# Split order of the seven-product MLP: block 6 loaded and split ahead of block 5

## The chip, the cores and the metric

The kernel runs on one core of one Trainium2 chip. The metric is device time in microseconds (us), the median of the runs shown. Beside the runs there is one profiled execution, whose trace all rows and durations here come from. The engines are TensorE (PE; PEld are its weight loads), VectorE (DVE), ScalarE (ACT), GpSimd (POOL) and SyncE (SP), which issues most DMAs.

## The reference

One layer of an encoder trunk on 512 rows of 1024 features: a mixer, a cross attention, and an MLP. The change is in the MLP alone:

```python
    u = rmsnorm(h, norm_ff_g[l]) @ w1[l]              # (512 x 1024) @ (1024 x 4096)
    h = h + jnp.square(jax.nn.relu(u)) @ w2[l]        # (512 x 4096) @ (4096 x 1024)
return rmsnorm(h, final_norm_g)
```

## The kernel before

The MLP's 4096 hidden features are cut into eight groups of 512. Group 0's up projection is computed in the plain way, which is the last thing before the loop that the change touches. For groups 1 to 7 (`SEVEN`) the up projection (`mlp_up7`), and for all groups the down projection (`mlp_down`), is a 2 x 2 block product made of **seven products** in place of eight. They are named 1 to 7, and TensorE computes them in the order of `PRODUCTS`: 1, 5, 6, 2, 7, 3, 4. In the loop a group's up stage comes first, then the down stage of the group before it; the last two groups share one down stage.

Every factor is held as two float32r tiles, a high part and the rest (`hi`, `lo`), and a product of factors is three matmuls: hi by hi, hi by the activations' rest, lo by hi. So each product of an up stage is 4 row blocks x 2 column halves x 3 = 24 matmuls of 128x256, and the third of them is the first that reads the weights' `lo`. A down stage has seven products of 12 matmuls of 128x512.

A **unit** is one weight block made ready for one product. `load` (line 1329) issues its DMA from SyncE into a raw tile `wru` (up) or `wrd` (down): for products 1, 2 and 3 straight from the weights, for 5, 6 and 7 from `wsu`/`wsd`, sums of blocks that GpSimd's adding DMAs ("presums", line 445, paced by TensorE's progress) have put into memory earlier. `prep` (line 1346) splits it: ScalarE copies it to `whu` (line 181), VectorE computes `wlu` = raw - `whu` (line 185). Product 4 has no load of its own: once block 6 is split, GpSimd adds a further block into the same raw tile (line 1356, the **adding DMA**), and that tile, split again, is block 4. Raw tiles, `wh`/`wl` tiles and PSUM banks are few, so a load or split often waits for an older tile's last reader.

In the up stage three PSUM banks hold the products: `uU` takes 1, then is copied to `uV` (line 1421) and takes 6 on top; `uY` takes 5, is saved as `y5` (line 1424), then overwritten with the sum in `uU` (`uY<-uU`, line 1426, after product 6) for product 3; `uU` takes 7 on top, VectorE reads it (`sq<-uU,y`, line 1430), and product 4 goes on top of it after that. So product 6 cannot start before the copy to `uV`, product 7 not before the copy `uY<-uU`, and product 4 not before line 1430.

`hidden_part` splits the hidden activations for the down stage into `hb` tiles (lines 1491 to 1495): `hb27` is group 2's for product 7. `hidden_sums` (lines 1476 to 1479) makes their sums `s5`, `n6`, `s3`, `s7` after product 4 of the up stage. `add_to` (lines 1508, 1510) adds down products to `acc`.

The order of the instructions on TensorE is the program's. On the other engines a scheduler sets it when the kernel is built, from the program's order, its own estimate of when operands are ready, and priorities: `ahead(PW)` raises or lowers an instruction's priority, `keep_in_program_order` fixes its place among its engine's instructions as written. Once built, each engine runs its queue strictly in that order, SyncE's DMA issues included. In the kernel before, block 4's split of the up stage and the copy `uY<-uU` are both kept in the program's order.

Of the kernel before, what the change touches and what calls it, by code (L numbers as in the profile page):

```python
# [12 lines left out]
AF = mybir.ActivationFunctionType  # L13
# [33 lines left out]
def emit(  # L47
# [21 lines left out]
    nc = tc.nc  # L69
    te, ve, ac, gp = nc.tensor, nc.vector, nc.scalar, nc.gpsimd  # L70
# [26 lines left out]
    def s4(shape, name, dt=F32):  # L97
        return s4p.tile([P] + shape, dt, tag="s4", name=name)

    def k4(shape, name, dt=F32):  # L100
        return k4p.tile([P] + shape, dt, tag="k4", name=name)
# [7 lines left out]
    def t2(name, dt=F32, shape=(S,)):  # L109
        return t2p.tile([P] + list(shape), dt, tag="t2", name=name)  # L110
# [6 lines left out]
    def mm(name, shape=(S,)):  # L117
        return mmp.tile([P] + list(shape), F32, tag="mm", name=name)
# [4 lines left out]
    def sc(name, shape=(S,)):  # L123
        return scp.tile([P] + list(shape), F32, tag="sc", name=name)
# [46 lines left out]
    def new_parts(shape, name):  # L171
        pad = [P, UK * (UW + FH)]
        hi = whp.tile([P, shape[0] * shape[1]], R, tag="wh", name=f"wh{name}", padded_shape=pad)
        lo = wlp.tile([P, shape[0] * shape[1]], R, tag="wl", name=f"wl{name}", padded_shape=pad)
        return [t.rearrange("p (k n) -> p k n", k=shape[0]) for t in (hi, lo)]

    def split_of(hi, lo, raw):
        def split(what="hl"):
            at = None
            if "h" in what:  # L180
                at = ac.activation(hi, raw, AF.Copy)  # L181
            if "v" in what:
                ve.tensor_copy(hi, raw)
            if "l" in what:
                ve.tensor_tensor(lo, raw, f(hi), ALU.subtract)  # L185
            return at

        return split
# [26 lines left out]
    def load_next(parts=2, between=None):  # L215

        i = len(stream)
        if i >= len(specs):
            return []
        units, splits = [], []  # L220
        uk = specs[i][0][1].shape[1] // 2
        for n in range(2):
            note = None if between is None else (lambda q, n=n: between(n * parts // 2 + q))
            unit, some = load_unit(f"{i}{'ab'[n]}", specs[i], slice(n * uk, (n + 1) * uk), parts // 2, note)
            units.append(unit)
            splits += some
        stream.append(tuple([u[x] for u in units] for x in range(2)))
        return splits
# [60 lines left out]
    def ahead(n):  # L289

        return tc.high_priority(offset=n) if n else nullcontext()
# [64 lines left out]
    first = load_next(4, more_x)  # L356
# [298 lines left out]
    for hp in range(2):  # L655
        wt = next_panel()
        for j in range(2):
            h = 2 * hp + j
            ps = mm(f"gq{h}")
# [124 lines left out]
    for li, m in enumerate(mlev):  # L784
# [8 lines left out]
        for hp in range(2):  # L793
# [3 lines left out]
            ps = sc(f"lv{hp}{m}", (NT, 2, w))  # L797
# [507 lines left out]
    for i in range(2):  # L1305
        gp.dma_start(gfin[i], final_norm_g[i * S : (i + 1) * S].partition_broadcast(P))
    HS = S // 2
    units, raws, unit_q = {}, {}, deque()
    sqs, comb, hbs = {}, {}, {}
    PRODUCTS = ("1", "5", "6", "2", "7", "3", "4")  # L1310
    QUAD = {"1": "00", "2": "10", "3": "11"}
    raw_n = [0]

    def raw_tile(name):
        raw_n[0] += 1
        if raw_n[0] % RAWS == 3:
            return t4(f"wr{name}")
        if raw_n[0] % RAWS in (0, 2):
            return wrp.tile([P, D], F32, tag="wr", name=f"wr{name}", padded_shape=[P, UK * UW])
        return s4([D], f"wr{name}")  # L1320
# [3 lines left out]
    def add_unit(key, shape):  # L1324

        kind, g, part = key[:3]
        name = "".join(map(str, key))
        block = block1 if kind == "u" else block2
        box = []

        def load():
            if part == "4":
                box.append(raws.pop((kind, g)))
                return
            if part == "6":
                raw = raws[kind, g] = s4(shape, f"wr{name}")
            else:
                raw = raw_tile(name).rearrange("p (k n) -> p k n", k=shape[0])
            if part in SUMS:
                src = wsum[kind, g, part]  # L1340
            else:
                src = block(g, QUAD[part])
            nc.sync.dma_start(raw, src)
            box.append(raw)

        def prep():
            while not box:
                load_q.popleft()()
            unit = new_parts(shape, name)
            late = (kind, part) == ("u", "4")  # L1350
            with ahead(0 if late else PW):
                split = split_of(unit[0], unit[1], box[0])()
                if late:
                    tc.keep_in_program_order(split)
            if part == "6":
                tc.keep_in_program_order(gp.dma_start(box[0], block(g, "10"), accum_op=ALU.add))  # L1356
            units[key] = unit

        unit_q.append((key, prep))
        load_q.append(load)  # L1360

    def up_units(g):
        for part in PRODUCTS:
            add_unit(("u", g, part), [UK, WT])

    def down_units(gs):
        for name in PRODUCTS:
            for g in gs:
                add_unit(("d", g, name), [2, S])

    def unit(*key):

        while key not in units:
            unit_q.popleft()[1]()
        got = units[key]
        at = order.index(key)
        while unit_q and len(order) - len(unit_q) < at + 4:
            unit_q.popleft()[1]()
        while load_q and len(order) - len(load_q) < at + LOADS:
            load_q.popleft()()  # L1380
        return got

    def square(ps, out_, sign=1.0):
        ac.activation(out_, ps, AF.Relu, scale=sign)
        ac.activation(out_, out_, AF.Square)
# [10 lines left out]
    def mlp_up7(g):  # L1396

        qa, qb = (k4([2, S], f"sq{g}{j}") for j in range(2))
        sqs[g, 0], sqs[g, 1] = qa, qb
        h1, h2 = slice(0, HS), slice(HS, S)  # L1400
        bank = {}

        for name in PRODUCTS:
            b = {"5": "Y", "3": "Y", "2": "V"}.get(name, "U")
            if b not in bank:
                bank[b] = (pvt if b == "Y" else mm)(f"u{b}{g}").rearrange("p (i n) -> p i n", i=2)
                if b == "V":
                    pass
            ps = bank[b]
            whi, wlo = unit("u", g, name)  # L1410
            xh, xl = xsum[name]
            for k in range(UK):
                for i in range(2):
                    ws, begin = slice(i * P, (i + 1) * P), name in "15" and k == 0 and i == 0
                    te.matmul(ps[:, i, :], whi[:, k, ws], xh[:, k, :], start=begin, stop=False, skip_group_check=True)  # L1415
                    te.matmul(ps[:, i, :], whi[:, k, ws], xl[:, k, :], start=False, stop=False, skip_group_check=True)  # L1416
                    at = te.matmul(ps[:, i, :], wlo[:, k, ws], xh[:, k, :], start=False, stop=k == UK - 1, skip_group_check=True)  # L1417
                presum.tick(6 * HS / 2400, at)
            if name == "1":
                bank["V"] = mm(f"uV{g}").rearrange("p (i n) -> p i n", i=2)  # L1420
                ac.activation(bank["V"], ps, AF.Copy)  # L1421
            elif name == "5":
                y5 = t2(f"y5{g}", F32, (2, HS))
                ac.activation(y5, ps, AF.Copy)
            elif name == "6":
                tc.keep_in_program_order(ac.activation(bank["Y"], ps, AF.Copy))
            elif name == "2":
                square(ps, qa[:, :, h1])
            elif name == "7":
                ve.tensor_tensor(qb[:, :, h2], ps, y5, ALU.add)  # L1430
                square(qb[:, :, h2], qb[:, :, h2], -1.0)
            elif name == "3":
                ve.tensor_tensor(qb[:, :, h1], ps, y5, ALU.add)
                square(qb[:, :, h1], qb[:, :, h1], -1.0)
            else:
                square(ps, qa[:, :, h2])
            yield
# [43 lines left out]

    hb_order = [(g, name) for g in range(NG - 2) for name in PRODUCTS]
    hb_order += [(g, name) for name in PRODUCTS for g in (NG - 2, NG - 1)]
    hb_used = [0]
# [37 lines left out]
    def mlp_down(gs):  # L1522

        end = gs[-1] == NG - 1
        banks = {}
        for n, name in enumerate(PRODUCTS):
            bank, first_, goes = PLAN[name]
# [123 lines left out]
    for g in range(1, NG):  # L1651
        up_units(g)
        if g < NG - 1:
            down_units((g - 1,))
# [88 lines left out]
```

## Time and profile before

| what | us |
|---|---|
| median of 3 runs | 761.11 |
| lowest, highest | 759.82, 763.25 |
| the profiled execution: its time | 764.39 |
| the profiled execution: span from first to last instruction | 762.7 |
| group loop, from group 1's first product to the last shared down stage | 452.9 to 717.4 of the span |

In a row of a time line the columns are start, duration, engine, line, operation, output<-inputs, shapes, a count where equal neighbours are merged, and in brackets the engine's idle time before it and what ended that. Buffer and group numbers are left out of names there: `wlu<-wru,whu` is some block's split of some group. Which one it is follows from its place in the queue. A row of the table of waits has the engine and line that waited, what it waited for, the total in us, how often, and the longest.

### The profile page before, as it was taken

To read this page: it belongs to the slowest core of one execution; us is meant where nothing else is said; L and a number is where in the kernel's file an instruction comes from. 1 tells how busy PE (TensorE), PEld (TensorE's weight loads), DVE (VectorE), ACT (ScalarE), POOL (GpSimd) and SP (SyncE) were. 2 spreads that over 40 slices of the span, in tenths; PEclk is the share of its full clock that TensorE was granted. 3 is DMA by queue.
4 is the path that set the end of the run, shared out by engine and by line. 5 is a ranking of instruction groups with operands and counts; after the bars stand their busy time and mean duration, and the time that the engine had idled before them with its cause. 6 is when DMAs were issued, how large, how long until landed. Compare 5 with 4: busy or idle time off the path is not lost.

```text
span 762.7 us, 12179 instructions
## 1 busy us (share of the span) xinstructions
PE 747.8 (98%) x4573; PEld 653.0 (86%) x4573; DVE 538.1 (71%) x849; ACT 432.6 (57%) x721; POOL 203.1 (27%) x278
## 2 busy tenths in 40 slices
PE   9999999999999999999999998989999999999996
PEld 6889888888889988888888888888989898999985
DVE  5647863677878656555546678968787887869697
ACT  5655554656666533244434459756574757575863
POOL 7207431323442246621021202111111111100033
PEclk9999999999999999999999999999999999999999
DMA  7541987577946899976569976997989889887452
GB/s 249 194 125 58 302 265 239 168 230 247 326 155 217 270 209 195 215 159 133 140 114 190 210 203 174 228 233 201 235 206 238 225 225 220 230 203 233 133 111 110
DMA packets 109965, 152.92 MB, mean 200 GB/s; under 512 B 6177, under 2 KB 75850, under 8 KB 109906
## 3 DMA queue, kind: packets, MB, share of 16 engines
q1 hardware_dynamic: 85314, 111.74, 45.0%
q0 software_dynamic: 24000, 39.35, 29.3%
q10 hardware_dynamic: 592, 1.05, 0.4%
q8 instruction: 36, 0.59, 0.3%
q14 instruction: 23, 0.19, 0.1%
HBM read 147.91 MB, written 51.40 MB: 261 GB/s over the span
## 4 chain that ended last, share of the span: by engine, by line
PE 73%; issue 8%; DMA 7%; ACT 6%; DVE 4%; POOL 1%; SPq 0%; POOLq 0%; ACTq 0%
DMA wru<-in_w_dram 5%; DMA wru<-wsu 2%; PE U L1543 2%; PE U L1542 2%; PE U L1544 2%; PE xq L254 2%; PE wo L254 2%; PE xq L255 2%; PE xq L256 2%; PE xw L254 2%; PE xw L255 2%; PE wo L255 2%; PE wo L256 2%; PE xw L256 2%; PE uU L1415 2%
## 5 line engine op out<-in xcount | busy, mean ns | idle before, releaser
L185 DVE TENSOR_TENSOR wlu<-wru,whu 128x1024 fp32r<-128x1024 f32 x49 | 58.7, 1218 | 39.1 <-ACT whu L181 39.1
L181 ACT ACTIVATE whu<-wru 128x1024 fp32r<-128x1024 f32 x49 | 51.6, 1055 | 56.5 <-DMA wru<-in_w_dram 23.0
L185 DVE TENSOR_TENSOR wld<-wrd,whd 128x1024 fp32r<-128x1024 f32 x56 | 68.3, 1221 | 13.8 <-ACT whd L181 13.8
L181 ACT ACTIVATE whd<-wrd 128x1024 fp32r<-128x1024 f32 x56 | 58.7, 1049 | 4.8 <-PE U L1544 2.1
L1542 PE MATMUL U<-whd,hb 128*128 128x512 f32 x120 | 46.8, 390 | 0.0
L1543 PE MATMUL U<-wld,hb 128*128 128x512 f32 x120 | 46.8, 390 | 0.0
L1544 PE MATMUL U<-whd,hb 128*128 128x512 f32 x120 | 46.7, 389 | 0.0
L1015 POOL TENSOR_SCALAR bi<-nF,Ft 128x128 f32<-128x128 f32 (+3 forms) x32 | 21.4, 676 | 59.5 <-PE pt L1047 36.3
L445 POOL DMA_DIRECT2D wsd<-in_w_dram x16 | 17.3, 1082 | 71.8 <-PE U L1544 13.7
L1415 PE MATMUL uU<-x_hi,whu 128*128 128x256 f32 x112 | 32.7, 292 | 3.4 <-DVE sq L1430 3.4
L1415 PE MATMUL uU<-xs_hi,whu 128*128 128x256 f32 x112 | 31.9, 285 | 2.5 <-ACT uV L1421 2.2
L1356 POOL DMA_DIRECT2D wru<-in_w_dram x7 | 9.3, 1328 | 89.5 <-DVE wlu L185 89.5
L1416 PE MATMUL uU<-x_lo,whu 128*128 128x256 f32 x112 | 32.4, 289 | 0.0
L1417 PE MATMUL uU<-x_hi,wlu 128*128 128x256 f32 x112 | 32.3, 289 | 0.0
L1415 PE MATMUL uY<-xs_hi,whu 128*128 128x256 f32 x112 | 31.7, 283 | 0.0
L1416 PE MATMUL uY<-xs_lo,whu 128*128 128x256 f32 x112 | 31.7, 283 | 0.0
L1417 PE MATMUL uU<-xs_hi,wlu 128*128 128x256 f32 x112 | 31.7, 283 | 0.0
L1416 PE MATMUL uU<-xs_lo,whu 128*128 128x256 f32 x112 | 31.7, 283 | 0.0
L1417 PE MATMUL uY<-xs_hi,wlu 128*128 128x256 f32 x112 | 31.7, 283 | 0.0
L1356 POOL DMA_DIRECT2D wrd<-in_w_dram x8 | 9.8, 1220 | 81.2 <-DVE wld L185 67.2
L445 POOL DMA_DIRECT2D wsu<-in_w_dram x14 | 17.6, 1259 | 47.6 <-PE xw L256 15.6
L1158 ACT ACTIVATE x_hi<-hT,gv 128x512 fp32r<-128x512 f32 x16 | 11.5, 716 | 27.5 <-DVE hT L1157 27.4
(965 smaller groups left out, 2662.6 us busy)
## 6 DMA issues: line engine op xcount, KB each, us to landing
wsd<-in_w_dram SPq DMA_DIRECT2D x24, 512.0 KB, 7.2
wrd<-in_w_dram SPq DMA_DIRECT2D x24, 512.0 KB, 7.4
wrd<-wsd SPq DMA_DIRECT2D x24, 512.0 KB, 4.9
wsu<-in_w_dram SPq DMA_DIRECT2D x21, 512.0 KB, 5.5
wru<-wsu SPq DMA_DIRECT2D x21, 512.0 KB, 6.4
wru<-in_w_dram SPq DMA_DIRECT2D x21, 512.0 KB, 5.6
wsd<-in_w_dram POOLq DMA_DIRECT2D x16, 512.0 KB, 7.2
wsu<-in_w_dram POOLq DMA_DIRECT2D x14, 512.0 KB, 8.4
```

The costliest lines, as they stand in the source:

```text
L181: at = ac.activation(hi, raw, AF.Copy)
L185: ve.tensor_tensor(lo, raw, f(hi), ALU.subtract)
L254: te.matmul(ps, wh, hi, start=n_ == 0 and not begun, stop=False)
L255: te.matmul(ps, wh, lo, start=False, stop=False)
L256: at = te.matmul(ps, wl, hi, start=False, stop=k == order[-1])
L445: yield gp.dma_start(wsum[kind, g, name], src, accum_op=ALU.add, **more)
L1415: te.matmul(ps[:, i, :], whi[:, k, ws], xh[:, k, :], start=begin, stop=False, skip_group_check=True)
L1416: te.matmul(ps[:, i, :], whi[:, k, ws], xl[:, k, :], start=False, stop=False, skip_group_check=True)
L1417: at = te.matmul(ps[:, i, :], wlo[:, k, ws], xh[:, k, :], start=False, stop=k == UK - 1, skip_group_check=True)
L1542: te.matmul(ps, hi, whi[:, k, :], start=begin, stop=False, skip_group_check=True)
L1543: te.matmul(ps, hi, wlo[:, k, :], start=False, stop=False, skip_group_check=True)
L1544: at = te.matmul(ps, lo, whi[:, k, :], start=False, stop=k == 1, skip_group_check=True)
```

## The change

It does four things. Block 6's unit comes ahead of block 5's in the list from which loads and splits are drawn (`SPLITS`); TensorE's order (`PRODUCTS`) stays. In `unit` the counts that decide how far to draw ahead are corrected by one for that swap. The splits of blocks 3 and 4 of an up stage lose their raised priority; in place of the program's order they get a dependency, within ScalarE's queue, on the copy `uY<-uU` of their group (`copyY`), and that copy is no longer kept in program order. The six loads of group 1's up stage keep the program's order on SyncE.

```diff
-    units, raws, unit_q = {}, {}, deque()
+    units, raws, copyY, unit_q = {}, {}, {}, deque()
     PRODUCTS = ("1", "5", "6", "2", "7", "3", "4")
+    SPLITS = ("1", "6", "5", "2", "7", "3", "4")
...
-            nc.sync.dma_start(raw, src)
+            dma = nc.sync.dma_start(raw, src)
+            if (kind, g) == ("u", 1):
+                tc.keep_in_program_order(dma)
             box.append(raw)
...
-            late = (kind, part) == ("u", "4")
+            late = kind == "u" and part in ("3", "4")
             with ahead(0 if late else PW):
                 split = split_of(unit[0], unit[1], box[0])()
                 if late:
-                    tc.keep_in_program_order(split)
+                    order_only = mybir.DependencyInfo(mybir.DependencyClass.NoSync, mybir.DependencyReason.DATA)
+                    tc.add_manual_dep(split.ins, copyY[g].ins.name, order_only, reason="copy first")
...
     def up_units(g):
-        for part in PRODUCTS:
+        for part in SPLITS:
             add_unit(("u", g, part), [UK, WT])
...
         at = order.index(key)
+        if key[0] == "u" and key[2] in ("5", "6"):
+            at = at - 1 if key[2] == "5" else at
...
             elif name == "6":
-                tc.keep_in_program_order(ac.activation(bank["Y"], ps, AF.Copy))
+                copyY[g] = ac.activation(bank["Y"], ps, AF.Copy)
```

What the built queues make of it, at three places. In names the first digit is the group and the second the product (`wru15`: raw block 5 of group 1); a number behind the underscore only tells buffers apart. The first place is SyncE's queue, the six loads of group 1's up stage, before:

```order
L1343 DMA wru15_4673<-wsu15_193 128x1024
L1343 DMA wru13_4772<-in_w1_dram 128x4x256
L1343 DMA wru12_4764<-in_w1_dram 128x4x256
L1343 DMA wru11_4667<-in_w1_dram 128x4x256
L1343 DMA wru16_4757<-wsu16_195 128x1024
L1343 DMA wru17_4770<-wsu17_194 128x1024
```

and now:

```order
L1344 DMA wru11_4667<-in_w1_dram 128x4x256
L1344 DMA wru16_4673<-wsu16_195 128x1024
L1344 DMA wru15_4758<-wsu15_193 128x1024
L1344 DMA wru12_4764<-in_w1_dram 128x4x256
L1344 DMA wru17_4770<-wsu17_194 128x1024
L1344 DMA wru13_4772<-in_w1_dram 128x4x256
```

Block 1, which TensorE needs first, was fourth and is first; block 5 was first and is third.

The second place is VectorE's queue ahead of group 3's product 5, before:

```order
L1495 TENSOR_TENSOR hb25_5581<-s5_2_5435,hb25_5581 128x512
L185 TENSOR_TENSOR wlu35_5562<-wru35_5470,whu35_5561 128x1024
L1508 TENSOR_TENSOR acc2_4315<-U10_5448,acc2_4315 128x512
L1508 TENSOR_TENSOR acc3_4316<-U11_5457,acc3_4316 128x512
L1493 SCALAR_TENSOR_TENSOR hb26_5603<-n6_2_5434,hb26_5603 128x512
L185 TENSOR_TENSOR wlu36_5585<-wru36_5495,whu36_5584 128x1024
L185 TENSOR_TENSOR wlu32_5610<-wru32_5518,whu32_5609 128x1024
```

and now:

```order
L1501 TENSOR_TENSOR hb25_5582<-s5_2_5435,hb25_5582 128x512
L185 TENSOR_TENSOR wlu36_5562<-wru36_5470,whu36_5561 128x1024
L1514 TENSOR_TENSOR acc2_4315<-U10_5448,acc2_4315 128x512
L1514 TENSOR_TENSOR acc3_4316<-U11_5457,acc3_4316 128x512
L1499 SCALAR_TENSOR_TENSOR hb26_5603<-n6_2_5434,hb26_5603 128x512
L185 TENSOR_TENSOR wlu35_5586<-wru35_5495,whu35_5585 128x1024
L185 TENSOR_TENSOR wlu32_5610<-wru32_5518,whu32_5609 128x1024
```

Blocks 5 and 6 have exchanged their places, and nothing else there has moved; groups 2 and 4 to 6 read alike, and in group 7 hb65 stands between them in place of hb26, and no hb row ahead of the first of them. ScalarE's `whu` rows are exchanged in the same way.

The third place is VectorE's queue at the start of a down stage, after group 2's product 4, before:

```order
L1476 TENSOR_TENSOR s5_2_5435<-sq21_5202,sq20_5201 128x512
L1477 TENSOR_TENSOR n6_2_5434<-s5_2_5435,sq20_5201 128x512
L1478 TENSOR_TENSOR s3_2_5437<-n6_2_5434,sq21_5202 128x512
L1479 TENSOR_TENSOR s7_2_5436<-sq20_5201 128x512
L1510 SCALAR_TENSOR_TENSOR acc2_4315<-Y10_5472,acc2_4315 128x512
```

and now:

```order
L1482 TENSOR_TENSOR s5_2_5435<-sq21_5202,sq20_5201 128x512
L1483 TENSOR_TENSOR n6_2_5434<-s5_2_5435,sq20_5201 128x512
L1501 TENSOR_TENSOR hb17_5488<-s7_1_5031,hb17_5488 128x512
L1484 TENSOR_TENSOR s3_2_5437<-n6_2_5434,sq21_5202 128x512
L1485 TENSOR_TENSOR s7_2_5436<-sq20_5201 128x512
L1516 SCALAR_TENSOR_TENSOR acc2_4315<-Y10_5472,acc2_4315 128x512
```

hb17 has come in; before, it stood some ten rows earlier, between the down block `wld11` and line 1430's `sq21`. On ScalarE it moved from the same place to behind the copy `V11<-U11` of the down stage's first product. It is so in groups 2 to 6; in group 1 hb07 stood at the start of the down stage already. In the up stages of all groups the splits of blocks 3 and 4 now stand behind the copy `uY<-uU` on ScalarE, and `hb` rows that stood behind that copy stand ahead of it: in group 1 uY follows uV, whu17, hb05, xs_hi, acc0, y5, hb06 and acc1, where whu13 and whu14 stood in place of hb06 and acc1.

## The prediction

> **What bounds the kernel now.** I read the page first, then the table of waits of TensorE, then the time line of each engine in the two stretches where TensorE waits.
>
> ```profile
> span 762.7 us, 12179 instructions
> PE 747.8 (98%) x4573; PEld 653.0 (86%) x4573; DVE 538.1 (71%) x849; ACT 432.6 (57%) x721; POOL 203.1 (27%) x278
> PE uU L1415 <- DVE sq L1430: 3.4, 5, 2.2
> PE uU L1415 <- ACT uV L1421: 2.2, 1, 2.2
> PE uU L1415 <- ACT uY L1426: 0.3, 1, 0.3
> ```
>
> The span is TensorE's. The change touches nothing before the group loop, so it can only win what TensorE loses between group 1's first product and the last stage. The three lines are its waits there: five before product 4 (total 3.4, longest 2.2 us), two in group 1. A wait as the table counts it begins at the modelled end of the last matmul; what it costs is the distance from start to start less the normal step. So I need the matmuls themselves (start, duration, engine, line, tile):
>
> ```profile
> 455.64 0.28 PE L1417 MATMUL uU<-x_hi,wlu 128*128 128x256 f32 x1
> 455.76 0.28 PE L1415 MATMUL uY<-xs_hi,whu 128*128 128x256 f32 x1
> 461.02 0.39 PE L1415 MATMUL uU<-xs_hi,whu 128*128 128x256 f32 x1 [2.22 <-ACT uV L1421]
> 467.37 0.39 PE L1415 MATMUL uU<-xs_hi,whu 128*128 128x256 f32 x1 [0.33 <-ACT uY L1426]
> 514.76 0.40 PE L1415 MATMUL uU<-x_hi,whu 128*128 128x256 f32 x1 [2.16 <-DVE sq L1430]
> 519.19 0.40 PE L1542 MATMUL U<-whd,hb 128*128 128x512 f32 x1
> 556.05 0.36 PE L1415 MATMUL uU<-x_hi,whu 128*128 128x256 f32 x1 [0.36 <-DVE sq L1430]
> ```
>
> The step is 0.12 us (455.64 to 455.76), so a product of 24 matmuls is 2.88 us. Product 5 of group 1 starts at 455.76 and product 6 should at 458.64; it starts at 461.02: 2.38 lost, and 0.10 on its slow first matmul. Product 7 should then start at 461.02 + 0.10 + 5.76 = 466.88, and starts at 467.37: 0.49, and 0.09. In groups 2 and 3 product 5 starts at 498.04 and 541.13 (two steps before the rows 498.28 and 541.37 below), so product 4, five products on, should start at 512.44 and 555.53. In group 2 it starts at 514.76: 2.32 lost. Its 24 matmuls then take 4.43 us (to 519.19) in place of 2.88, 1.55 more; the next view says why. In group 3 it starts at 556.05: 0.52, and 0.06. Groups 4 to 6 look like it: of the table's 3.4 us the longest takes 2.2, which leaves 1.2 to four waits, and each costs some 0.16 more than the table says (0.52 against 0.36) and 0.07 after it: 1.2 + 4 x 0.23 = 2.1 for groups 3 to 6. Sum: 2.48 + 0.58 + 3.87 + 2.1 = **9.0 us**. More than this can't be won.
>
> ```profile
> 511.51:514.92 3.41, 1.25 (x11) 1.08 (x10) 2.71 (x4) 2.63 (x5) 0.00 (x0) 1.00 0.75 188
> 514.92:518.33 3.41, 3.41 (x17) 3.41 (x17) 2.65 (x3) 3.08 (x5) 0.00 (x0) 0.50 0.42 152
> 456.90:460.30 3.40, 1.90 (x16) 1.70 (x15) 3.37 (x3) 3.40 (x7) 1.34 (x1) 1.00 0.29 34
> 521.93:541.74 19.81, 19.81 (x103) 16.99 (x102) 19.74 (x28) 11.07 (x14) 0.90 (x1) 1.00 0.95 260
> ```
>
> These are stretches: length, busy time of PE, PEld, DVE, ACT, POOL, then the granted TensorE clock. Behind the 2.32 us wait of group 2 the clock is 0.50 for 3.41 us, which is the 1.55. In group 1 the wait of 2.38 us drew no such thing. The last row is for later: VectorE is busy 19.74 of 19.81 us.
>
> **Product 4's wait, removed.** It ends on VectorE (POOL and ScalarE rows first, then VectorE's, group 3):
>
> ```profile
> 530.56 0.90 POOL L445 DMA_DIRECT2D wsu<-wsu  x1 [9.84 <-DMA wru<-wsu]
> 542.03 1.34 POOL L1356 DMA_DIRECT2D wru<-in_w_dram  x1 [10.56 <-DVE wlu L185]
> 550.46 1.06 ACT L181 ACTIVATE whu<-wru 128x1024 fp32r<-128x1024 f32 x1 [2.73 <-DMA wru<-in_w_dram]
> 537.58 1.22 DVE L185 TENSOR_TENSOR wlu<-wru,whu 128x1024 fp32r<-128x1024 f32 x1
> 540.52 1.22 DVE L185 TENSOR_TENSOR wlu<-wru,whu 128x1024 fp32r<-128x1024 f32 x1
> 551.55 1.23 DVE L185 TENSOR_TENSOR wlu<-wru,whu 128x1024 fp32r<-128x1024 f32 x1 [4.55 <-ACT whu L181]
> 552.70 1.22 DVE L185 TENSOR_TENSOR wld<-wrd,whd 128x1024 fp32r<-128x1024 f32 x1
> 555.22 0.68 DVE L1430 TENSOR_TENSOR sq<-uU,y 128x512 f32<-128x512 f32 x1
> ```
>
> Block 6's split ends at 541.74, GpSimd issues the adding DMA at 542.03, it is there at 550.46, block 4 is split on ScalarE, then on VectorE, then wld, hb27, and only then the sq that frees U, at 555.90; TensorE starts 0.15 later. The change gives block 6 the place of block 5 (537.58): the DMA starts 2.94 us earlier less 0.5 (below). hb27, which kept VectorE from sq31 until 555.22, leaves that place. The chain then ends before 553, and sq31 waits for product 7 alone, which ends at 552.65 (555.53 less 2.88): done by 553.5 for a start at 555.53. In group 2 the slack is smaller but there: 514.6 less 2.9 for the earlier DMA and less 0.6 for the hb row is 511.1 against 512.44. So 3.87 + 2.1 = **6.0 us goes**, the half clock with it.
>
> **Product 5's wait, new.** The same swap puts block 5's split into block 6's place (540.52 in group 3), and product 5 comes before product 6 on TensorE. Its third matmul is the first that reads wlu.
>
> ```profile
> 498.28 0.28 PE L1417 MATMUL uY<-xs_hi,wlu 128*128 128x256 f32 x1
> 498.93 1.22 DVE L185 TENSOR_TENSOR wlu<-wru,whu 128x1024 fp32r<-128x1024 f32 x1
> 541.37 0.28 PE L1417 MATMUL uY<-xs_hi,wlu 128*128 128x256 f32 x1
> 581.17 0.28 PE L1417 MATMUL uY<-xs_hi,wlu 128*128 128x256 f32 x1
> 580.39 1.22 DVE L185 TENSOR_TENSOR wlu<-wru,whu 128x1024 fp32r<-128x1024 f32 x1
> 700.40 0.28 PE L1417 MATMUL uY<-xs_hi,wlu 128*128 128x256 f32 x1
> 699.01 2.35 DVE L185 TENSOR_TENSOR wlu<-wru,whu 128x1024 fp32r<-128x1024 f32 x2
> 521.93 0.69 DVE L1476 TENSOR_TENSOR s<-sq,sq 128x512 f32<-128x512 f32 x1 [0.34 <-ACT sq L1385]
> 522.65 0.69 DVE L1477 TENSOR_TENSOR n<-s,sq 128x512 f32<-128x512 f32 x1
> 523.38 0.69 DVE L1478 TENSOR_TENSOR s<-n,sq 128x512 f32<-128x512 f32 x1
> 561.86 0.69 DVE L1476 TENSOR_TENSOR s<-sq,sq 128x512 f32<-128x512 f32 x1 [0.29 <-ACT sq L1385]
> ```
>
> In groups 2, 3, 4 and 7 these are that third matmul and the place that block 5 gets. From s5 (521.93) to the end of that split (541.74) VectorE is full, by the last row of the stretches, so nothing lets block 5 come sooner, and the run grows: the change moves hb17 between n6 and s3. hb17 can start at 523.26 (n6's 523.34 less the usual overlap of 0.08), lasts 0.69 and lets s3 start at 523.89, not 523.38: +0.51. In groups 4 to 7 s5 comes 2.87 us after the down products start (561.86 less 556.05 + 2.94), in group 3 2.74 (521.93 - 519.19); with product 4's wait gone I take 2.74 for all, so there +0.51 - 0.13 = +0.38. With 0.15 us from VectorE to TensorE, product 5 waits:
> - group 3: 540.52 + 1.22 + 0.51 + 0.15 - 541.37 = 1.03
> - group 4: 580.39 + 1.22 + 0.38 + 0.15 - 581.17 = 0.97; the same for 5 and 6, whose up and down stages have the same rows
> - group 7: 699.01 + 1.22 + 0.38 + 0.15 - 700.40 = 0.36
> - group 2: 498.93 + 1.22 + 0.15 - 498.28 = 2.02. No hb is inserted ahead of it, and ScalarE, which sets s5 of group 1, comes up to 0.5 us sooner against TensorE (next part): between 1.5 and 2.0, I take 1.75.
>
> Sum 1.75 + 1.03 + 2.91 + 0.36 = 6.05, and 0.08 for each of six slow first matmuls: **6.5 us comes**. Bounds: VectorE's hb17 hidden and s5 0.3 us sooner throughout gives 4; a further op of 0.69 us in each run gives 10.
>
> **Group 1.** Product 6 waits for the copy uV, which stands in ScalarE's queue:
>
> ```profile
> 429.87 3.64 SPq L1343 DMA_DIRECT2D wru<-in_w_dram  x3
> 433.01 11.43 DMA wru<-in_w_dram
> 445.62 1.22 DVE L185 TENSOR_TENSOR wlu<-wru,whu 128x1024 fp32r<-128x1024 f32 x1 [4.52 <-ACT whu L181]
> 453.41 1.06 ACT L1464 ACTIVATE xs_hi<-xs_d 128x1024 fp32r<-128x1024 f32 x1 [1.11 <-DVE xs_d L1461]
> 460.39 0.58 ACT L1421 ACTIVATE uV<-uU 128x512 f32<-128x512 f32 x1
> ```
>
> Block 1's load was issued at 433.01, behind those of 5, 3 and 2, and arrived at 444.44; VectorE's queue stood 4.52 us behind it, and with it xs_d and ScalarE's xs_hi of 453.41, from which ScalarE has no idle time until uV. In program order it is the first of the six, out before block 5's, which was ahead of the three issues of 429.87; even at 11.4 us it is there by 441, when VectorE's wait of 4.52 us begins. xs_d then runs 4.5 us sooner. ScalarE gains less, since ahead of that xs_hi stands the square of u010, which waits for TensorE: group 1 starts at 452.88 (455.76 less 2.88), u011 before it has 24 steps of 0.227 (19.06 us for the 84 matmuls of a down stage, 519.19 to 541.37 less 3.12), so u010 is done at 447.4. With 0.2 for the hand-over and 2.2 for three operations behind it (two of 0.6 and one of 1.0, as such tiles take in these rows) xs_hi comes at 449.8, 3.6 sooner, and uV at 456.8, done at 457.4 for a product 6 at 458.64. uY now stands behind whu17, hb05, xs_hi, acc0, y5, hb06 and acc1 in place of two splits more; these seven take about 5.5 us and uY 0.6, so it is ready at 463.5 for a product 7 at 464.4. So **3.1 us goes**; if the queue keeps a late piece up to 0.6 stays. Blocks 7 and 3 now stand behind block 2's load, which was out by 433 (429.87 + 3.64); they are split 20 us later and more.
>
> **Sum.** -6.0 - 3.1 + 6.5 = -2.6 us on the profiled 762.7, that is 760.1. The profiled execution is 1.6 us above the median of the runs shown (761.11), so **758.5 us**, 0.3% faster.
>
> **Rivals.**
> A. Product 5 does not wait: VectorE catches up, because its run has less to do than I count. Against it: the full stretch 521.93 to 541.74. Halfway (waits of 0.4) it is 9.0 - 2.5 = 6.5 faster, 754.6; wholly, 752.1.
> B. The half clock moves to group 2's new wait. For: 2.32 us drew it there. Against: 2.38 did not in group 1, where TensorE was busy 1.90 of the 3.40 us before 460.30, against 1.25 of 3.41 in group 2; the new wait is below 2.1 us, so at least 1.3 of such a stretch stays busy. It costs 3.41 x 0.5 = 1.7: 760.2. [...]
> C. The slower side: the half clock follows every new wait of 1 us and more, in groups 2 to 6. Five times 1.7 is 8.5, so 767. It decides from the point at which 1 us of idle time is enough; the 0.52 and 0.49 us waits drew none.
> D. The adding DMA starts sooner but lands no sooner, since a presum's DMA shares GpSimd's queue. Then product 4's 6.0 stay and the new 6.5 come on top of them, less 3.1: 764.5. Against: GpSimd's issue before 542.03 is that of 530.56, and the next stands behind it.
>
> **How the numbers follow.** Chances: forecast 0.52, A 0.25, B 0.10, C 0.05, D 0.08. The forecast's own range is 757 to 760.5 (group 2 at 1.5 or 2.0, the hb row 0.3 either way in five groups, 0.6 in group 1). Taking in B and most of A: 754.5 to 762.5. What a measurement can tell from no change is about 0.5%, 3.8 us: faster is below 757.3. That is nearly all of A and a tenth of the forecast, 0.29; slower is C and a third of D, 0.08; the rest, 0.63, lies between.
>
> **What would show it.** In the changed profile: TensorE's waits name wlu (L185) before uY's third matmul, in groups 2 to 7, near 1 us and largest in group 2; no waits for sq L1436, uV or uY; VectorE without idle time from s5 to block 5's split. No wait before uY means A; a clock of 0.50 in the group loop means B or C; sq again means D.

## The result and the profile after

Over 22 runs each, the change takes 760.60 us (760.06 to 760.98) and the kernel before 763.67 us (758.95 to 768.60): a ratio of 0.996, 95% interval 0.9946 to 0.9975, so 3.07 us or 0.4% faster. The three runs of before shown ahead of the prediction (761.11) lay on its lower side. In the profiled executions the span falls from 762.7 to 758.9 us.

The page of the changed kernel and its table of waits of TensorE in the group loop (engine, line, what it waited for, total us, times, longest):

```profile
span 758.9 us, 12210 instructions
PE 746.1 (98%) x4573; PEld 650.7 (86%) x4573; DVE 539.4 (71%) x849; ACT 434.4 (57%) x721; POOL 203.4 (27%) x278
PE uY L1423 <- DVE wlu L185: 4.0, 5, 1.1
```

One line stands in place of three: no wait for uV, uY or sq is left, and a new one has come, for `wlu`. The time line of TensorE at these places (start, duration, engine, line, operation, tiles, shapes, idle time and releaser):

```profile
452.91 0.28 PE L1421 MATMUL uU<-x_hi,whu 128*128 128x256 f32 x1
467.30 0.28 PE L1421 MATMUL uY<-xs_hi,whu 128*128 128x256 f32 x1
...
496.55 0.39 PE L1423 MATMUL uY<-xs_hi,wlu 128*128 128x256 f32 x1 [1.15 <-DVE wlu L185]
510.80 0.28 PE L1421 MATMUL uU<-x_hi,whu 128*128 128x256 f32 x1
...
536.73 0.38 PE L1423 MATMUL uY<-xs_hi,wlu 128*128 128x256 f32 x1 [0.71 <-DVE wlu L185]
550.98 0.28 PE L1421 MATMUL uU<-x_hi,whu 128*128 128x256 f32 x1
```

In group 1 the sixth product starts 14.39 us after the first, five products of 2.88 without a gap. In groups 2 and 3 product 5's third matmul (496.55, 536.73) comes 1.30 and 0.87 us after its step; product 4 (510.80, 550.98) starts without a wait, and no half clock follows: the granted clock is 1.00 from 448 to 752.3 us. Counted the same way, from start to start less the step, slow matmuls included, TensorE's losses in the loop are:

| group | before | after |
|---|---|---|
| 1, products 6 and 7 | 2.48 + 0.58 | 0 |
| 2, product 4 with the half clock | 3.87 | 0 |
| 3 to 6, product 4 | 2.2 | 0 |
| 2, product 5 | 0 | 1.40 |
| 3 to 6, product 5 | 0 | 4 x 0.97 |
| 7, product 5 | 0 | 0.37 |
| sum | 9.1 | 5.65 |

(Groups 3 to 6 are counted one by one here; the prediction took 2.1 from the table of waits.) The 3.5 us between the sums are the difference of the spans (3.8) but for 0.3, and that stands behind the last matmul: from its end to the end of the span it is 6.83 us before and 6.47 after. Why this tail is shorter was not traced.

### The profile page after: what moved, and what is told of

It is laid out like the page before. It is cut to its first block, busy times and chain, and to the rows that moved or that the text cites. A ratio compares the mean times of both kernels' runs of the same rounds, so it can differ in the third digit from the quotient of the medians.

```text
span 758.9 us, 12210 instructions
## 1 busy us (share of the span) xinstructions
PE 746.1 (98%) x4573; PEld 650.7 (86%) x4573; DVE 539.4 (71%) x849; ACT 434.4 (57%) x721; POOL 203.4 (27%) x278
## 4 chain that ended last, share of the span: by engine, by line
PE 93%; DVE 3%; ACT 1%; issue 1%; POOL 1%; DMA 1%; SPq 0%; ACTq 0%; POOLq 0%
PE U L1548 4%; PE U L1549 4%; PE U L1550 4%; PE uU L1421 3%; PE uU L1422 3%; PE uU L1423 3%; PE uY L1423 2%; PE xq L254 2%; PE wo L254 2%; PE xq L255 2%; PE xw L254 2%; PE xq L256 2%; PE xw L256 2%; PE wo L256 2%; PE xw L255 2%; PE Y L1550 2%
## 5 line engine op out<-in xcount | busy, mean ns | idle before, releaser
L1497 ACT ACTIVATE hb<-sq 128x512 fp32r<-128x512 f32 x24 | 15.1, 631 | 25.2 <-DVE wlu L185 9.1
```

## The experiments

Each kernel ran beside the kernel before: the first four experiments on one chip (the kernel before took 763.86 us there), the last four on another (764.07 us). "Lost" is the sum of TensorE's losses in the group loop in the profiled execution; the ratio is to the kernel before, with its 95% interval.

| kernel | median us (range, runs) | ratio | span | lost | span less lost |
|---|---|---|---|---|---|
| the change | 760.60 (760.06 to 760.98, 22) | 0.9960 (0.9946 to 0.9975) | 758.9 | 5.65 | 753.2 |
| load order alone | 759.80 (759.04 to 767.37, 12) | 0.9956 (0.9932 to 0.9980) | 757.5 | 4.5 | 753.0 |
| the change, no load order | 763.62 (760.32 to 766.43, 12) | 0.9987 (0.9963 to 1.0011) | 762.2 | 8.9 | 753.3 |
| the change, block 5 early | 755.23 (754.87 to 755.37, 5) | 0.9871 (0.9845 to 0.9897) | 753.2 | 0 | 753.2 |
| the change, adding DMA late | 761.88 (760.83 to 763.23, 12) | 0.9968 (0.9947 to 0.9988) | 759.1 | 6.5 | 752.6 |
| load order, no swap, block 6 early | 755.25 (754.95 to 755.75, 5) | 0.9882 (0.9866 to 0.9898) | 754.0 | 0 | 754.0 |
| the change, old late rule | 760.51 (759.84 to 761.04, 6) | 0.9951 (0.9938 to 0.9965) | 759.0 | 5.7 | 753.3 |
| the change, block 5 behind block 2 | 769.56 (768.34 to 770.66, 4) | 1.0070 (1.0051 to 1.0089) | 767.0 | 13.9 | 753.1 |
| the change, block 5 behind blocks 2 and 7 | 783.01 (1 run) | | 781.3 | 28.3 | 753.0 |

The last column tests the whole reading: 752.6 to 754.0 us remain after the loop's losses. The 1.4 us between these lie outside the loop. From group 1's first product to the end of the last matmul, less the losses, it is 293.8 to 293.9 us in all nine kernels and in the kernel before; group 1's first product starts at 452.3 to 453.2 us, and behind the last matmul stand 6.5 us in the kernels with the swap and 6.8 to 6.9 in the three without. So within the loop these executions differ, to 0.1 us, by what TensorE loses there alone. The swap's split order and its corrected counts were always run together; which of the two does what is not known.

### Group 1's load order alone

In the kernel before:

```diff
-            nc.sync.dma_start(raw, src)
+            dma = nc.sync.dma_start(raw, src)
+            if (kind, g) == ("u", 1):
+                tc.keep_in_program_order(dma)
```

> The kernel before with one part of the change alone: group 1's loads keep the program's order on SyncE. Theory (the parts add): TensorE's waits for uV and uY in group 1 (2.48 and 0.58 us in the profile before) go, and nothing else changes: five waits for sq before product 4, the longest 2.3 us in group 2 with the half clock behind it (1.55 us), stay. Span 762.7 - 3.1 = 759.6, about the time of the whole change (its profiled span is 758.9), since the rest of the change took 6.0 and gave 5.65 back. Rival 1 (part of group 1's waits hangs on the new place of block 6 as well): uV or uY stays with 0.5 us or more, span 760 to 761. Rival 2 (the half clock depends on where a 3.41 us window falls on the wait): group 2's wait stays at 2.3 us and its half clock goes, span 758.0. The spread over the runs stays as wide as before's (758.95 to 768.6), since product 4's waits hang on the landing of a DMA; if it becomes as narrow as that of the whole change (760.06 to 760.98), group 1 made it.

Its table of waits and its longest wait:

```profile
PE uU L1417 <- DVE sq L1432: 3.2, 5, 1.4
510.37 0.36 PE L1417 MATMUL uU<-x_hi,whu 128*128 128x256 f32 x1 [1.38 <-DVE sq L1432]
496.21 1.32 POOL L1358 DMA_DIRECT2D wru<-in_w_dram  x1 [9.94 <-DVE wlu L185]
504.78 1.06 ACT L181 ACTIVATE whu<-wru 128x1024 fp32r<-128x1024 f32 x1 [3.75 <-DMA wru<-in_w_dram]
```

Both waits of group 1 are gone, so the first rival falls. The span is 757.5 us, 2.1 below the theory's: group 2's wait shrank as well, from 2.32 to 1.54 us, and drew no half clock, which no theory had. With product 5 starting at 494.43, the adding DMA is issued 1.78 us after it, in place of 2.40 in the kernel before (500.44, 498.04), and is there 8.57 us later in place of 8.73. The order of group 1's loads thus reaches into group 2. The runs still spread over 8.3 us. By its median this one part is no worse than the whole change.

### The change without the load order

The same three lines taken out of the change.

> The whole change without the kept order of group 1's loads. Theory: block 1's load is issued behind those of other blocks again, TensorE waits for uV 2.4 us and for uY 0.5 us in group 1, and groups 2 to 7 are as with the whole change (waits of 1.4, 0.97 four times and 0.36 before product 5's third matmul, none for sq): span 758.9 + 3.1 = 762.0. Rival 1 (the late rule for block 3 moves the copy uY forward and so covers group 1's second wait): 761.4 to 761.5, with uV's wait alone. Rival 2 (block 6's earlier split helps group 1 too): no wait there, 758.9. If the runs spread over more than 3 us, group 1 is what spreads before's; if within 1.5 us, product 4's waits are.

```profile
PE uY L1421 <- DVE wlu L185: 5.2, 6, 2.0
PE uU L1419 <- ACT uV L1425: 1.2, 1, 1.2
499.92 0.39 PE L1421 MATMUL uY<-xs_hi,wlu 128*128 128x256 f32 x1 [1.99 <-DVE wlu L185]
```

Group 1 loses 2.35 us again, now at its own product 5 (0.51) and at product 6 (1.36), while product 7 starts only 0.17 us late. Group 2's product 5 waits 2.15 us where it waits 1.30 with the load order. The span is 762.2, as the theory had it, in other shares: 2.35 of the 3.2 us come back in group 1 and 0.85 in group 2. By the interval the swap without the load order gains nothing that can be measured. With product 4's waits gone the runs still spread over 6.1 us. The expectation's either-or was too narrow: with the load order alone group 1's waits are gone, and the runs spread over 8.3. So neither is the only cause of the spread.

### Block 5 early on VectorE

```diff
-            with ahead(0 if late else PW):
+            with ahead(0 if late else PW + 100 * ((kind, part) == ("u", "5"))):
```

> The whole change, and on VectorE block 5's second half is split ahead of the last pair of additions to acc and of hb6's second half in each of groups 2 to 7 (on ScalarE hb2 and y5's copy change places; nothing else moves). Theory (product 5's new wait is only its place behind 1.96 us of rows that nothing waits for, 1.28 + 0.68): the split ends at 494.7 in place of 496.49 in group 2 and 534.9 in place of 536.67 in group 3; all six waits (sum 5.65 us) go, TensorE has no wait left in the loop, span 753.2 to 753.5, median 755, ratio to before 0.989. Rival 1 (VectorE's full run only passes the delay on: the additions or hb6 hold up block 2's split or the next down stage): the wait moves to product 2 or to the first down product, 0.5 us or more in each group, span 756 to 758. Rival 2 (ScalarE's half of the split, done at 531.30 in group 3, or the first product is the bound): waits of 0.3 to 0.5 stay before product 5, span 755 to 756.

VectorE ahead of group 3's product 5, and TensorE at its third matmul:

```profile
531.02 2.35 DVE L185 TENSOR_TENSOR wlu<-wru,whu 128x1024 fp32r<-128x1024 f32 x2
533.29 1.28 DVE L1514 TENSOR_TENSOR acc<-U,acc 128x512 f32<-128x512 f32 x2
534.49 0.68 DVE L1499 SCALAR_TENSOR_TENSOR hb<-n,hb 128x512 fp32r<-128x512 f32 x1
535.09 2.35 DVE L185 TENSOR_TENSOR wlu<-wru,whu 128x1024 fp32r<-128x1024 f32 x2
535.44 0.28 PE L1423 MATMUL uY<-xs_hi,wlu 128*128 128x256 f32 x1
```

Blocks 6 and 5 are split in one go (531.02, x2), so block 5 follows block 6 by 1.14 us in place of 2.94, 1.8 sooner, and TensorE's table of waits has no row in the loop. The theory's span of 753.2 came to the tenth, both rivals fall, and the additions and hb6, now 1.14 us later, hold up nothing. This kernel is faster than both the kernel before (0.9871 of its time) and the change (5.4 us below).

### The adding DMA late

The up stage's adding DMA is written behind block 5's split, with a dependency on it (`last_lo[0]` is VectorE's latest split):

```diff
-            if part == "6":
+            if part == "6" and kind == "u":
+                held[g] = box[0]
+            elif part == "6":
                 tc.keep_in_program_order(gp.dma_start(box[0], block(g, "10"), accum_op=ALU.add))
+            if part == "5" and kind == "u":
+                add = gp.dma_start(held.pop(g), block(g, "10"), accum_op=ALU.add)
+                sync = mybir.DependencyInfo(mybir.DependencyClass.Sync, mybir.DependencyReason.DATA)
+                tc.add_manual_dep(add.ins, last_lo[0].ins.name, sync, reason="add behind 5")
+                tc.keep_in_program_order(add)
```

> The whole change, but the DMA that adds to block 6's buffer is issued only when VectorE has split block 5, 2.9 us later, as late as in the kernel before; every row of VectorE and ScalarE stays as the change has it. Theory of the prediction (group 2's wait went because the DMA starts earlier; the row hb7 alone is worth 0.6): product 4 of group 2 waits 1.6 us again, perhaps with the half clock's 1.5 us behind it, span 760.5 to 762; groups 3 to 6 stay without a wait. Rival (counted again from the profile of the change): the DMA would land 8.7 us after 496.8, the split on ScalarE and VectorE, wld and sq follow without the hb7 row between them, sq is done at about 509.5, and product 4 is due at 510.8, because product 5's new wait has pushed it back 1.4 us: no wait, span 758.9 to 759.2. Then the earlier DMA was not what removed the wait, but the hb7 row that left and the delay that the new wait makes.

Group 2's chain (GpSimd's issue, block 4's halves, sq, product 4) and group 7's product 4:

```profile
496.20 1.32 POOL L1366 DMA_DIRECT2D wru<-in_w_dram  x1 [9.94 <-DVE wlu L187]
505.28 1.06 ACT L183 ACTIVATE whu<-wru 128x1024 fp32r<-128x1024 f32 x1 [1.89 <-DMA wru<-in_w_dram]
506.38 1.23 DVE L187 TENSOR_TENSOR wlu<-wru,whu 128x1024 fp32r<-128x1024 f32 x1 [1.73 <-ACT whu L183]
508.65 0.69 DVE L1445 TENSOR_TENSOR sq<-uU,y 128x512 f32<-128x512 f32 x1
510.23 0.28 PE L1430 MATMUL uU<-x_hi,whu 128*128 128x256 f32 x1
711.30 0.36 PE L1430 MATMUL uU<-x_hi,whu 128*128 128x256 f32 x1
```

The same chain of group 2 in the kernel before:

```profile
500.44 1.32 POOL L1356 DMA_DIRECT2D wru<-in_w_dram  x1 [10.56 <-DVE wlu L185]
509.17 1.06 ACT L181 ACTIVATE whu<-wru 128x1024 fp32r<-128x1024 f32 x1 [4.53 <-DMA wru<-in_w_dram]
513.32 0.69 DVE L1495 TENSOR_TENSOR hb<-s,hb 128x512 fp32r<-128x512 f32 x1 [0.69 <-ACT hb L1491]
513.92 0.68 DVE L1430 TENSOR_TENSOR sq<-uU,y 128x512 f32<-128x512 f32 x1
```

Group 2 has no wait: sq ends at 509.34, product 4 starts at 510.23 as due. Most of this is the rival. Three things cover the late DMA there: it is still issued 0.62 us sooner against product 5 than in the kernel before (1.78, as with the load order alone); from the start of `whu` to the end of sq it takes 4.06 us in place of 5.44, since the row hb17 (0.69) and VectorE's wait of 0.69 for ScalarE's half of it are gone; and the new wait makes product 4 due 1.4 us later. Without the last of the three group 2 would wait: sq ends 0.89 us before product 4 starts. Small waits come back, too: 0.08, 0.12 and 0.25 us at product 4 in groups 4, 5 and 7, and the median is 1.3 us above the change's with a spread of 2.4. So with the change's own new wait in place the earlier issue is no condition, but margin. It gives more than the 2.9 us of the issue, since the DMA also lands sooner after it: in groups 2 to 7 it takes 6.1 to 7.1 us in the change, 8.1 to 8.7 in the kernel before and 9.0 to 9.9 here (496.20 to 505.28 in group 2). What slows the late one was not traced.

### No swap: block 6 early instead

In the kernel with the load order alone:

```diff
-            with ahead(0 if late else PW):
+            with ahead(0 if late else PW + 100 * ((kind, part) == ("u", "6"))):
```

> The kernel before with the kept load order of group 1, no swap and no new late rule; in place of the swap, VectorE splits block 6's second half ahead of the last pair of additions to acc and of hb6's second half in groups 2 to 7, so that the adding DMA starts 1.96 us earlier than in the run with the load order alone, whose waits before product 4 were 1.54, 0.85, 0.56, 0.43, 0.59 and 0.07 us (span 757.5). Theory (product 4's waits hang on the chain from the adding DMA, and any way of starting it 2 us earlier will do, without a wait at product 5): all of them go, 4.47 us with the slow matmuls behind them, span 753.0, median near 755, as with the swap and block 5 early (755.2). Rival (in groups 3 to 6 it is the row hb7 ahead of sq that counts, and it stays where it was): waits of 0.4 to 0.6 stay there, span 755 to 756, and the runs spread over 2 us and more.

Group 3's adding DMA, and VectorE ahead of its product 4:

```profile
533.73 1.34 POOL L1358 DMA_DIRECT2D wru<-in_w_dram  x1 [8.84 <-DVE wlu L185]
542.15 1.23 DVE L185 TENSOR_TENSOR wlu<-wru,whu 128x1024 fp32r<-128x1024 f32 x1 [1.72 <-ACT whu L181]
546.29 0.69 DVE L1497 TENSOR_TENSOR hb<-s,hb 128x512 fp32r<-128x512 f32 x1 [0.70 <-ACT hb L1493]
546.89 0.68 DVE L1432 TENSOR_TENSOR sq<-uU,y 128x512 f32<-128x512 f32 x1
```

No row of waits in the loop, as the theory had it, and 755.25 us, against 755.23 with the swap and block 5 early. The profiled span is 754.0, 1.0 above the theory; group 1's first product starts 0.9 us later here than with the load order alone, and the loop itself agrees to 0.1. The hb7 row still stands right ahead of sq and costs nothing now: an earlier DMA is enough by itself, and the swap, with the wait that it brings, was not needed for it. A way for sq past hb7, with neither an earlier DMA nor a wait at product 5, was not run.

### The late rule of before

The change with `late = (kind, part) == ("u", "4")` and both `keep_in_program_order` lines of the kernel before.

> The whole change with the late rule of the kernel before: only block 4's split is kept behind the copy uY in the program, and by the resulting order ScalarE makes the copy uY behind the splits of blocks 3 and 4 in groups 2 to 6, two rows later (VectorE's rows differ in group 1 alone). Theory (the rule changes nothing that TensorE waits for): block 4's buffer is there 8.4 us after the DMA is issued at 534.0 in group 3, its split ends by 543.5 to 544.1, the copy 0.6 later, and product 7 is due at 545.2: span 758.9, median 760.6, a spread of 1 us. Rival (the copy now waits for the adding DMA, and a landing over 0.5 us late reaches TensorE): waits for uY in some groups, median 761 to 762.5, a spread of 2 us and more, as with the DMA issued late (760.83 to 763.23).

ScalarE's copy in group 3:

```profile
543.51 0.58 ACT L1431 ACTIVATE uY<-uU 128x512 f32<-128x512 f32 x1
```

It ends at 544.09, 1.25 us ahead of product 7's start. The median is 760.51 us, with a spread of 1.2 and losses of 5.7: the theory. That hb17 moved is thus the swap's doing, not this rule's, and the rule is worth nothing that could be measured here.

### Longer waits at product 5

Block 5's second half is split behind block 2's; in a second kernel, with `part == "7"` in the last condition, behind block 7's as well:

```diff
+                later = kind == "u" and g > 1 and part == "5"
+                split = split_of(unit[0], unit[1], box[0])
+                if later:
+                    held[g] = split
+                split = split("h" if later else "hl")
+                if kind == "u" and part == "2" and g in held:
+                    behind = last_lo[0]
+                    held.pop(g)("l")
+                    no_sync = mybir.DependencyInfo(mybir.DependencyClass.NoSync, mybir.DependencyReason.DATA)
+                    tc.add_manual_dep(last_lo[0].ins, behind.ins.name, no_sync, reason="five behind")
```

> The whole change, with the second half of block 5 split one row later still on VectorE, behind that of block 2, in groups 2 to 7: each wait before product 5's third matmul grows by 1.14 us, to 2.44 in group 2, 2.0 in groups 3 to 6 and 1.4 in group 7. Without a half clock the span is 758.9 + 6 x 1.14 = 765.7. Theory (the clock is set by how much of a window of 3.41 us TensorE was busy: 1.25 us brought the half, 1.90 did not): a wait of 2.0 leaves at least 1.4 busy, so groups 3 to 6 draw none, and group 2's wait, which can leave 0.97, does so only when it falls inside one window: span 765.7, or 767.3. Rival (a wait of some 2 us is enough wherever it falls): a half clock behind each of groups 2 to 6, 1.5 to 1.7 us each, span 773 to 774.

> The same with block 5's second half behind those of blocks 2 and 7: waits of 3.58 us in group 2, 3.15 in groups 3 to 6, 2.54 in group 7. Without a half clock the span is 758.9 + 6 x 2.28 = 772.6. Theory (what counts is the busy part of a window, with the bound between 1.25 and 1.90 of 3.41 us): a wait of 3.15 leaves less than 1.25 in one window unless the window's edge cuts it near the middle, so two thirds of the six, about four, draw a half clock of 1.5 to 1.7 us: span 777 to 781. Rival (the bound is on the length of the wait, over 3.4 us): group 2 alone draws one, span 774.

Stretches of 3.41 us, the length of the half clocks in these profiles (514.92 to 518.33 in the kernel before), counted from where the clock changes; the expectations call them windows (length, busy time of PE, PEld, DVE, ACT, POOL, granted clock, DMA share, GB/s). With block 5 behind block 2, groups 2, 3 and 4:

```profile
495.91:499.33 3.42, 1.79 (x15) 1.79 (x16) 2.72 (x4) 1.21 (x3) 0.00 (x0) 1.00 1.09 182
536.88:540.29 3.41, 1.57 (x14) 1.43 (x13) 3.06 (x3) 1.67 (x3) 0.00 (x0) 1.00 1.02 160
540.29:543.70 3.41, 3.41 (x19) 3.41 (x18) 0.69 (x1) 0.92 (x2) 0.94 (x1) 0.50 1.06 344
577.83:581.25 3.42, 1.99 (x17) 1.78 (x15) 3.42 (x5) 1.54 (x2) 2.49 (x2) 1.00 0.79 234
```

and behind blocks 2 and 7, groups 2, 3 and 7:

```profile
493.47:496.89 3.42, 1.61 (x14) 1.40 (x12) 3.42 (x5) 1.54 (x2) 1.32 (x1) 1.00 0.96 307
537.84:541.26 3.42, 0.23 (x3) 0.11 (x2) 3.30 (x4) 1.98 (x3) 0.00 (x0) 1.00 1.07 174
541.26:544.67 3.41, 3.41 (x17) 3.41 (x18) 0.44 (x1) 0.00 (x0) 0.79 (x1) 0.50 0.97 298
715.34:718.75 3.41, 1.01 (x8) 1.01 (x9) 2.35 (x2) 0.44 (x1) 0.00 (x0) 1.00 1.10 238
```

In the first kernel the waits are 2.44, 2.0 four times and 1.40 us, and there is one half clock in the loop: behind group 3's 2.0 us, all of which lies in one stretch (1.57 busy), and not behind group 2's 2.44, which lies across two (1.79 busy in the poorer one). The span, 767.0, is the theory's with one half clock; that it is group 3's and not group 2's is not. In the second, five of the six waits draw one, groups 3 to 7 (3.35 us each, group 7's also, which was expected at 2.54); group 2's, the longest at 3.58, draws none; it lies across two stretches with 1.61 and 1.80 us busy. That is one more half clock than expected, and the span of 781.3 lies just above the theory's 777 to 781. Length alone does not decide (2.0 us drew one, 3.58 us none), so both rivals fall. The change without the load order adds a stretch from the other side: its wait of 2.15 us in group 2 drew no half clock.

```profile
498.09:501.51 3.42, 1.59 (x13) 1.59 (x14) 3.42 (x5) 1.07 (x2) 0.46 (x1) 1.00 0.81 150
```

Its loop has no change of clock to count from; the drop to 0.50 behind its last matmul (760.92) is used. In the kernel before, that drop (760.68) lies 72 times 3.413 us behind the half clock's start (514.92); that it does so here as well is the author's assumption.

## Why the prediction was right, and where its sizes were off

**The forecast's mechanism held in each of its three terms**: 9.1 us of losses gone, where 9.0 were counted, a new wait at product 5 in groups 2 to 7, a small gain left over. By the trace -9.1 + 5.65 = -3.5, against -2.6 predicted. The absolute 758.5 stood on a median of three runs, which lay 2.56 us below that of the 22; set against the latter, the same -2.6 gives 761.1 for the 760.60 measured. As it stands, 760.60 lies 0.1 above the forecast's own range (757 to 760.5) and inside the wider one (754.5 to 762.5). The step from 760.1 to 758.5 also set a span (762.7) against a time (761.11); the profiled execution's own time is 764.39, 3.3 above that median. This slip moves nothing, since 758.5 is 761.11 less 2.6.

**Product 4's wait.** All of the 6.0 us went, and as forecast `sq` then waits for product 7 alone. Group 2 of the change (the adding DMA, blocks 3 and 4 on ScalarE, sq):

```profile
493.85 1.32 POOL L1360 DMA_DIRECT2D wru<-in_w_dram  x1 [7.01 <-DVE wlu L185]
502.92 2.00 ACT L181 ACTIVATE whu<-wru 128x1024 fp32r<-128x1024 f32 x2
508.12 0.69 DVE L1436 TENSOR_TENSOR sq<-uU,y 128x512 f32<-128x512 f32 x1 [0.63 <-PE uU L1423]
```

The sum had more margin than it knew. In group 2 the earlier DMA (2.9) had to carry it, with 0.6 for the hb row. The hb row is worth 1.38, more than twice as much, the DMA lands 7.0 us after its issue in place of 8.7, and two covers were missing from the sum, 0.62 from the load order and 1.4 from the change's own new wait; so the DMA issued late brings no wait back there. What the earlier issue does buy is 1.3 us in the median and a narrow spread.

**Product 5's wait.** 5.65 in place of 6.5. The run of VectorE in the changed kernel, from s5 of group 2 to block 5's split of group 3:

```profile
516.42 0.69 DVE L1482 TENSOR_TENSOR s<-sq,sq 128x512 f32<-128x512 f32 x1 [0.34 <-ACT sq L1391]
517.14 0.69 DVE L1483 TENSOR_TENSOR n<-s,sq 128x512 f32<-128x512 f32 x1
517.78 0.69 DVE L1501 TENSOR_TENSOR hb<-s,hb 128x512 fp32r<-128x512 f32 x1
518.39 0.69 DVE L1484 TENSOR_TENSOR s<-n,sq 128x512 f32<-128x512 f32 x1
...
534.86 0.68 DVE L1499 SCALAR_TENSOR_TENSOR hb<-n,hb 128x512 fp32r<-128x512 f32 x1
535.46 3.49 DVE L185 TENSOR_TENSOR wlu<-wru,whu 128x1024 fp32r<-128x1024 f32 x3
```

The first of the three splits at 535.46 is block 5's; it ends at 536.67, and TensorE's matmul starts at 536.73. hb17 stands between n6 and s3 as predicted and costs 0.52, where 0.51 was taken: s3 starts 1.97 us behind s5, in place of 1.45. The start of s5, 2.74 us behind the down stage's first matmul, came as taken too, in groups 3 to 7. The term that was too large there is the hand-over to TensorE: 0.06, not the 0.15 of sq and product 4. In group 3 the run grew by 0.44 alone (20.25 us from s5 to the end of the split, 19.81 before), because one pair of additions had taken 0.07 longer before:

```profile
526.92 1.35 DVE L1510 SCALAR_TENSOR_TENSOR acc<-U,acc 128x512 f32<-128x512 f32 x2
```

In the change the same pair takes 1.28. That is 1.03 less 0.16, the 0.87 measured. In group 2 the load order counted for more than was taken: s5 of group 1 starts 18.11 us ahead of product 5 before and 18.73 in the change, 0.62 sooner, where the prediction took a quarter of a microsecond and allowed 0.5. So the wait of 1.30 came out below its own lower bound of 1.5. (Without the load order it is 2.15.)

**Group 1.** The 3.1 us went, and by the load order alone, as the run with only that part shows. The path was right as well: in the change `xs_hi` starts at 449.73, the copy `uV` ends at 457.27 and `uY` at 463.28, where 449.8, 457.4 and 463.5 were forecast.

**The rivals.** A (no wait at product 5) did not come about in the change, but its price was right: all of the 9.0 us off the profiled span is 753.7, and with block 5 split 1.8 us sooner the span is 753.2. B and C (a half clock behind the new waits) did not come, but the reason given against B, that at least 1.3 us of a stretch stay busy, was not enough: a stretch with 1.57 us busy was followed by one in the kernel with block 5 behind block 2. There a wait of 2.0 us was enough, so the upper end of the forecast's 1.5 to 2.0 for group 2 was not clear of it. The wait came out at 1.30, with the clock at 1.00 behind it, by the load order's 0.62 that the forecast had too small: in this it was lucky. The longer waits show how near B and C were: one row of VectorE more, 1.14 us, turns the 0.4% gain into a loss of 0.7% (0.5 to 0.9%), with 13.9 us lost in the loop in place of 5.65, one half clock among them. D fell: in group 2 the adding DMA was issued at 493.85 and landed 7.0 us later, and block 4's ScalarE half, the second of the pair at 502.92, started at 503.87 behind block 3's, not behind the DMA.

**The half clock.** Of the stretches of 3.41 us counted out in the group loop of four profiles, those with TensorE busy for 0.23 to 1.57 us (group 2 of the kernel before, group 3 with block 5 behind block 2, groups 3 to 7 with it behind blocks 2 and 7) had a half clock behind them, and those with 1.59 us and more had none. A wait of 2.0 us inside one stretch drew one, and a wait of 3.58 us across two did not. That the busy part of such a stretch is what counts is the author's reading of these rows; what sets the clock is not shown.

## What to carry to other kernels

When a transfer hangs behind a split, moving that split ahead of rows with no reader nearby (here additions and an hb row, 1.8 us) cost nothing, while exchanging it with another split that TensorE reads sooner only moved the wait: 0.4% against 1.2 to 1.3%, all with the load order. Look in the full engine's queue for the rows that nobody waits for, not for a partner to swap with. And test each part of a change by itself: here the load order alone gained as much as the whole change, and the swap alone nothing that could be measured.

## What was not expected

The change narrowed the runs' spread from 9.65 us to 0.92. It takes both parts: with the load order alone it is 8.3 us, with the swap alone 6.1, and 0.5 and 0.8 us (five runs each) in the two kernels in which TensorE has no wait left in the loop. Half clocks have a part in it, as the granted clock noted for each run shows. Of the kernel before's runs beside the first four experiments, the ten at a mean clock of 0.998 or 0.999 took 759.7 to 764.0 us, and those at 0.993 to 0.995 took 763.5 us or more; the change's 22 runs all stand at 0.997 to 0.999. That a DMA's landing, which ends the waits before product 4, differs from run to run is the likely other part. It is not shown, since only one execution of each kernel was traced.
